# Turning the gated FFN tiles by DMA instead of by TensorE

## The chip, the cores and the metric

The kernel runs on one NeuronCore of one Trainium2 chip. The metric is the device time of one execution in microseconds (us), lower is better; the median of the runs shown is compared. The core has a matrix engine (TensorE, "PE" in the profile, with its weight loads listed apart as "PEld"), VectorE ("DVE"), ScalarE ("ACT"), GpSimd ("POOL"), and SyncE ("SP"), which here only issues DMAs. Sixteen DMA engines move data for all of them. Each engine works through its own instructions in a fixed order and waits at an instruction until that instruction's inputs and output buffer are ready, so what stands behind a waiting instruction on the same engine waits with it.

## The reference

The kernel computes an encoder of two layers on 512 tokens with 1024 channels, float32:

```
for l in range(DEPTH):                                  # DEPTH = 2
    x = x + 0.5 * swiglu(rms_norm(x, ffn1_norm[l]), ffn1_w_in[l], ffn1_w_out[l])
    x = x + mixer(rms_norm(x, mix_norm[l]), ...)
    x = x + 0.5 * swiglu(rms_norm(x, ffn2_norm[l]), ffn2_w_in[l], ffn2_w_out[l])
return rms_norm(x, final_norm)

def swiglu(x, w_in, w_out):
    g, u = jnp.split(x @ w_in, 2, axis=-1)              # D_FF = 2816 columns each
    return (jax.nn.silu(g) * u) @ w_out
```

There are therefore four SwiGLU feed-forward stages (two per layer) and two mixers (neighbourhood attention and a Fourier mix). The change concerns only what lies between `silu(g) * u` and the second product in the four feed-forward stages.

## The kernel before, in words

**Products.** Every float32 matrix is split into a high part (float32r, rounded by a ScalarE copy) and a low part (a VectorE subtraction), and each product is three TensorE products of parts. On top of that the products are done by Strassen's scheme, seven products of quarter matrices (numbered 1 to 7 in the code) in place of eight.

**Weights.** `Stream` walks a list of weight granules of 128 by 1024 floats (512 KB). SP loads a granule into a buffer `raw` (line 147); for some, POOL adds a second granule to it by an accumulating DMA (line 149); VectorE sums pairs for others (line 163). ScalarE then writes the high part `whi` (line 190, or 185 for a negated one) and VectorE the low part `wlo` (line 193 or 186). There are nine `raw` buffers in a feed-forward stage, and three each of `whi` and `wlo`; loads are asked for eight granules ahead, the split two ahead of the product that uses it. A granule serves twelve matmuls in a feed-forward stage.

**A feed-forward stage.** `stage_ffn` has an input half and an output half. The input half goes over the 2816 columns in five blocks of 512 (`for jb in range(...)`; in three of the stages the first block is `first_block`), and one block of 256 columns besides. A block runs the products in the order 1, 5, 6, 2, 7, 3, 4. ScalarE copies partial sums out of PSUM (`snap`, line 560), VectorE subtracts (`less`, line 565), ScalarE takes the tanh (`gate`, line 695), and VectorE multiplies gate and up part (`times`, line 702). The results of a block are two tiles `z2` and `z1`, each [128 tokens, 2 token blocks, 512 columns]: `z2` for tokens 256 to 511, `z1` for tokens 0 to 255. Both are ready only around the last product of the block.

**The turn.** The output half needs the gated values with columns on the partitions. `late_at` remembers each finished `z`. `settle_at` calls `to_at`, which turns a 128 by 128 piece by a TensorE transpose against the identity (line 613), four pieces into one PSUM bank `tr`, and ScalarE copies that bank into an `at` tile (line 617, or line 620 where the two column groups belong to different `at` tiles). One `z` takes eight transposes. In a block of the loop `settle_at` stands between products 1 and 5 (inside `two`), and for the last block after the first product of the output half (`if i == 0`). `at_tile(h, j, c)` gives twelve tiles per stage; `PLACE` says in which one a group of 128 columns goes.

**The output half.** 21 products (`steps`: factors 1 and 2, then 5, 6, 7, 3, and 4, three chunks each) take `at` tiles, or VectorE sums of them (line 715), split into high and low parts by `make`, two steps ahead. VectorE adds the results to `x` (line 721).

**Buffers and order.** Work tiles of 4 KB per partition come from one pool of 23 (`slot`). Outside the blocks marked `manual_schedule`, the order on each engine is fixed before the run by a planner that plays the program through with its own durations: on an engine that is free it places the instruction that comes first in the program among those whose inputs it takes to be ready. On the chip that order then stays as it is, whatever the real durations are. DMAs on SP's and POOL's queues are ordered in the same way.

Of the kernel before, what the change touches and what calls it, by code (L numbers as in the profile page):

```python
# [10 lines left out]
F32R = mybir.dt.float32r  # L11
BF16 = mybir.dt.bfloat16
I32 = mybir.dt.int32
AF = mybir.ActivationFunctionType
ALU = mybir.AluOpType
AX = mybir.AxisListType

P = 128
# [20 lines left out]
PLACE = {f: (h, c, i) for h in range(2) for c in range(3) for i, f in enumerate(CHUNK[h][c])}  # L39
# [50 lines left out]
def encoder_kernel(  # L90
    ctx: ExitStack, tc: tile.TileContext, xin, xtr, wst, gains, gfin, gbias, bias_in, dft, chan, ident_in, rot, out
):
    nc = tc.nc
    V, S, G, PE = nc.vector, nc.scalar, nc.gpsimd, nc.tensor
# [15 lines left out]
    def slot(dt=F32, s="k", shape=(4, 256)):  # L110
        return kp.tile([P, *shape], dt, tag="k", name=nm(s), bufs=23)
# [383 lines left out]
    def product(ps, acts, kts, start, stop=True, again=False, hook=None, by_block=False, ahead=AHEAD):  # L495

        h, l, off = acts
        n = (len(kts) + 1) // 2  # L500

        def granule(i, w, b):
            res = []
            for k, kt in enumerate(kts[2 * i : 2 * i + 2]):
                c, z = slice(off + b * P, off + (b + 1) * P), slice(k * T, (k + 1) * T)
                res.append((
                    ps[b], h[:, kt, c], l[:, kt, c], w[0][:, z], w[1][:, z], start and i + k == 0,
                    stop and 2 * i + k == len(kts) - 1,
                ))
            return res  # L510

        if by_block:
            w = [ws.next() for _ in range(n)]
            for b in range(2):
                for i in range(n):
                    late_low(granule(i, w[i], b), again)
            return
        for i in range(n):
            w = ws.next(AHEAD if i < n - 1 and ahead else ahead)
            if i < n - 1:  # L520
                late_low(granule(i, w, 0) + granule(i, w, 1), again)
            else:
                late_low(granule(i, w, 0), again)
                late_low(granule(i, w, 1), again)
            if hook and i == 0:
                hook()

    def product_T(ps, acts, start):


        h, l, off = acts
        c = slice(off, off + 256)
        wh, wl = ws.next()
        for part in range(2):
            for m in range(2):
                to = ps[:, m * 256 : (m + 1) * 256]
                for k in range(4):
                    z = slice(k * 256 + m * P, k * 256 + (m + 1) * P)
                    if part:
                        PE.matmul(to, wl[:, z], h[:, k, c], start=False, stop=k == 3, skip_group_check=True)  # L540
                    else:
                        one = start and m == 0 and k == 0
                        PE.matmul(to, wh[:, z], h[:, k, c], start=one, stop=False, skip_group_check=True)
                        PE.matmul(to, wh[:, z], l[:, k, c], start=False, stop=False, skip_group_check=True)
# [52 lines left out]
    def stage_ffn(norm, nxt, late):  # L597
# [4 lines left out]
        def at_tile(h, j, c):  # L602
            if (h, j, c) not in at:
                at[h, j, c] = slot(F32, "at")
            return at[h, j, c]
# [42 lines left out]
        if first:  # L648
            for g in range(2):
                w = ws.next()  # L650
# [7 lines left out]
            with tc.manual_schedule(engines={mybir.EngineType.DVE, mybir.EngineType.Activation}):  # L658
# [11 lines left out]
                norm.squares(0, 1)  # L670
                norm.squares(1, 1)
                split(*t4, b21)
        late_at = []
        def plain_out():
            for j in range(2):
                th = slot(F32, "th", (2, 256))
# [10 lines left out]
        def settle_at():  # L687
            while late_at:
                to_at(*late_at.pop(0))
# [9 lines left out]
        def times(z, u, j):  # L699
            for b in range(2):  # L700
                c = 2 * j + b
                V.scalar_tensor_tensor(z[:, b, :], u[b], norm.r2[:, c : c + 1], z[:, b, :], ALU.mult, ALU.mult)
# [64 lines left out]
        def half_times(g, r, u, to, j):  # L767
            V.tensor_tensor(to, u, r, ALU.mult)
            V.tensor_tensor(at_tile(0, j, 0)[:, 0:2, :], g, to, ALU.mult)

        def first_block():

            f0 = 2

            def snap_T(ps):
                t = slot(F32, "sn", (2, 256))
                S.activation(t, ps.rearrange("p (m t) -> p m t", m=2), AF.Copy)
                return t

            def less_T(ps, t):  # L780
                V.tensor_tensor(t, ps.rearrange("p (m t) -> p m t", m=2), t, ALU.subtract)

            pa, ha = pair("A"), bank("hA")
            product(pa, acts[1], K4, True)
            combine(5)
            s1 = snap(pa)
            if len(norm.due) == 2:
                norm.quad(*norm.due.pop(0))
            product_T(ha, acts[1], True)
            h1 = snap_T(ha)  # L790
            pb, hb = pair("B"), bank("hB")
            product(pb, acts[5], K4, True)
            combine(6)
            sb = snap(pb)
            norm.settle()
            product_T(hb, acts[5], True)
            hsb = snap_T(hb)
            norm.rstd()
            norm.spread(R)
            product(pa, acts[6], K4, False, again=True)  # L800
            s2 = snap(pa)
            combine(7)
            product_T(ha, acts[6], False)
            h2 = snap_T(ha)
            pc = pair("C")
            product(pc, acts[2], K4, True)
            less(pc, s1)
            combine(4)
            z1 = gate(s1, 0)
            product(pa, acts[7], K4, False, again=True)  # L810
            hc = bank("hC")
            product_T(hc, acts[2], True)
            less_T(hc, h1)
            r1 = half_gate(h1, 0)
            less(pa, sb)
            product_T(ha, acts[7], False)
            less_T(ha, hsb)
            product(pb, acts[3], K4, False, again=True)
            less(pb, s2)
            z2 = gate(s2, 1)  # L820
            times(z2, [sb[:, 0, :], sb[:, 1, :]], 1)
            product_T(hb, acts[3], False)
            less_T(hb, h2)
            r2 = half_gate(h2, 1)
            half_times(h2, r2, hsb, hsb, 1)
            product(pa, acts[4], K4, False, again=True)
            times(z1, pa, 0)
            product_T(ha, acts[4], False)
            half_times(h1, r1, ha.rearrange("p (m t) -> p m t", m=2), h2, 0)
            late_at.extend([(z2, 1, f0, 4), (z1, 0, f0, 4)])  # L830

        if not first:
            R = slot(F32, "R", (2, T))[:, 0, :]
# [1 line left out]
        for jb in range(0 if first else 1, NB):  # L835
            f0 = 2 + 4 * jb
            if first and jb == 0:
                with tc.manual_schedule(engines={mybir.EngineType.DVE, mybir.EngineType.Activation}):
                    pa = pair("A")
                    product(pa, acts[1], K4, True)  # L840
                    for j in range(2):
                        t = snap(pcl[j])
                        pcl[j] = [t[:, 0, :], t[:, 1, :]]
                    s1 = snap(pa)
                    second(s1)
                    pb = pair("B")
                    product(pb, acts[5], K4, True)
                    sb = snap(pb)
                    norm.rstd()
            else:  # L850
                pa, pb, s1, sb = two(jb)
                settle_at()
            product(pa, acts[6], K4, False, again=True)
            s2 = snap(pa)
            settle_at()
            if jb or not first:
                second(s1)
            else:
                plain_out()
            z1 = gate(s1, 0)  # L860
            product(pa, acts[7], K4, False, again=True)
            less(pa, sb)
            product(pb, acts[3], K4, False, again=True)
            less(pb, s2)
            z2 = gate(s2, 1)
            times(z2, [sb[:, 0, :], sb[:, 1, :]], 1)
            if jb == NB - 1:
                make(0)
                make(1)
            product(pa, acts[4], K4, False, again=True)  # L870
            times(z1, pa, 0)
            late_at += [(z2, 1, f0, 4), (z1, 0, f0, 4)]

        if late or nxt.mix:
            tc.keep_in_program_order(S.activation(small("sq", 1), ones, AF.Sqrt))
# [1 line left out]
        for i, (m, c, _) in enumerate(steps):  # L877
# [13 lines left out]
            )  # L891
            if i == 0:
                settle_at()
            if m == 4 and c == 0 and not late:
                with tc.manual_schedule(engines={mybir.EngineType.DVE, mybir.EngineType.Activation}):
                    make(i + 2)
                    nxt.quad(1, 1)
                    if nxt.mix:
                        nxt.low01 = nxt.quad_high(0, 1)
                    else:  # L900
                        nxt.quad(0, 1)
# [1044 lines left out]
```

## Time and profile before

| | |
|---|---|
| median of 3 runs | 1898.24 us (1897.55 to 1899.96) |
| span of the profiled execution, first to last instruction | 1896.1 us |
| median minus span | 2.1 us |
| mean granted TensorE clock | 0.999 |
| busy share of the span: PE, PEld | 99%, 83% |
| busy share of the span: DVE, ACT, POOL | 87%, 63%, 9% |
| DMA queue of SP / of POOL, share of 16 engines | 41.7% / 28.5% |

Of the profiled execution the profile gives only the span; its own time with what lies around it is not listed, so the median of the runs stands in for it: what lies around the span is taken as 2.1 us. The feed-forward stages lie at about 10 to 337, 605 to 925, 925 to 1265 and 1550 to 1890 us; their input halves end at about 230, 838, 1166 and 1778 us.

How to read it: an engine that is busy all the time sets the end if the others keep it fed. A busy share over the whole span is a mean over stages with different limits, so the tables by stage count more. "Idle before" and the lists of waits say how long an engine sat and whose signal ended it. The chain that ended last is followed backwards from the last instruction: a piece of work on it costs its length, one beside it nothing.

### The profile page before, as it was taken

How to read it: one execution, taken by the hardware profiler on the slowest of the kernel's cores; microseconds unless marked ns; L12 is line 12 of the kernel's file. 1: busy time of each engine (PE TensorE's matmuls, PEld its weight loads, DVE VectorE, ACT ScalarE, POOL GpSimd, SP SyncE). 2: the span in 40 equal slices, each digit the busy share in tenths (PEclk: the TensorE clock that was granted, in tenths of full speed). 3: DMA queues.
4: the chain of work that ended last, by engine and by line, in shares of the span. 5: the costliest groups of instructions: out<-in, count | busy, mean ns of one | idle time of the engine just before them, and what ended most of it. 6: DMA issues, size and time to landing. Idle time of an engine off the chain costs nothing.

```text
span 1896.1 us, 25080 instructions
## 1 busy us (share of the span) xinstructions
PE 1883.8 (99%) x9150; PEld 1578.6 (83%) x9150; DVE 1647.4 (87%) x2006; ACT 1188.6 (63%) x1700; POOL 171.5 (9%) x210
## 2 busy tenths in 40 slices
PE   9999999999999999999999999999999999999998
PEld 7888888888888888888888888888888888888886
DVE  7877899788989987889998778998889899887899
ACT  6655665668665755566665556666685576556664
POOL 0101011100111010001010100101001101100010
PEclk9999999999999999999999999999999999999999
DMA  9777498932886777649867764988248867766594
GB/s 302 208 201 189 152 244 262 230 102 98 242 219 163 183 191 204 178 151 258 254 193 202 194 174 154 267 267 213 84 137 229 215 169 177 207 177 178 173 278 143
DMA packets 106940, 372.75 MB, mean 197 GB/s; under 512 B 12288, under 2 KB 12416, under 8 KB 106816
## 3 DMA queue, kind: packets, MB, share of 16 engines
q1 hardware_dynamic: 78144, 272.80, 41.7%
q0 software_dynamic: 28528, 98.33, 28.5%
q8 instruction: 72, 1.18, 0.2%
q14 instruction: 52, 0.43, 0.1%
q10 hardware_dynamic: 144, 0.02, 0.0%
HBM read 365.85 MB, written 2.11 MB: 194 GB/s over the span
## 4 chain that ended last, share of the span: by engine, by line
PE 96%; DMA 1%; DVE 1%; issue 1%; SPq 0%; ACT 0%; POOL 0%; DVEq 0%; POOLq 0%; ACTq 0%
PE A L490 10%; PE A L491 10%; PE A L493 10%; PE o L493 7%; PE o L490 7%; PE o L491 7%; PE B L490 5%; PE B L491 5%; PE B L493 5%; PE ps L314 4%; PE ps L315 4%; PE ps L316 3%; PE C L491 2%; PE C L490 2%; PE C L493 2%; PE tr L613 2%
## 5 line engine op out<-in xcount | busy, mean ns | idle before, releaser
L190 ACT ACTIVATE whi<-raw 128x1024 fp32r<-128x1024 f32 (+1 forms) x534 | 551.4, 1037 | 388.5 <-PE A L491 124.2
L193 DVE TENSOR_TENSOR wlo<-raw,whi 128x1024 fp32r<-128x1024 f32 (+1 forms) x534 | 633.3, 1192 | 167.7 <-ACT whi L190 166.4
L149 POOL DMA_DIRECT2D raw<-in_wst_dram x166 | 144.4, 899 | 1369.9 <-DMA raw<-in_wst_dram 927.9
L163 DVE TENSOR_TENSOR raw<-raw,raw 128x1024 f32<-128x1024 f32 (+1 forms) x150 | 177.4, 1190 | 1.2
L490 PE MATMUL A<-whi,xh 128*128 128x512 f32 x400 | 155.7, 389 | 0.0
L491 PE MATMUL A<-whi,xl 128*128 128x512 f32 x400 | 155.7, 389 | 0.0
L493 PE MATMUL A<-wlo,xh 128*128 128x512 f32 x400 | 115.1, 389 | 0.0
L185 ACT ACTIVATE whi<-raw 128x1024 fp32r<-128x1024 f32 (+1 forms) x83 | 85.8, 1037 | 42.2 <-PE o L491 14.0
L186 DVE SCALAR_TENSOR_TENSOR wlo<-raw,whi 128x1024 fp32r<-128x1024 f32 (+1 forms) x83 | 98.0, 1194 | 12.7 <-ACT whi L185 12.7
L695 ACT ACTIVATE th<-sn,rh 128x512 f32<-128x512 f32 x80 | 56.9, 715 | 69.7 <-DVE sn L565 69.7
L560 ACT ACTIVATE sn<-A 128x512 f32<-128x512 f32 x104 | 60.8, 589 | 45.8 <-PE A L493 45.7
L493 PEld LDWEIGHTS A<-wlo,xh 128*128 128x128 f32 x400 | 75.1, 188 | 15.6
L491 PEld LDWEIGHTS A<-whi,xl 128*128 128x128 f32 x400 | 75.1, 188 | 15.4
L490 PEld LDWEIGHTS A<-whi,xh 128*128 128x128 f32 x400 | 75.1, 188 | 15.4
L490 PE MATMUL C<-whi,xh 128*128 128x512 f32 x208 | 81.2, 390 | 0.0
L491 PE MATMUL C<-whi,xl 128*128 128x512 f32 x208 | 81.0, 389 | 0.0
L490 PE MATMUL B<-whi,xh 128*128 128x512 f32 x208 | 81.0, 389 | 0.0
L491 PE MATMUL B<-whi,xl 128*128 128x512 f32 x208 | 81.0, 389 | 0.0
L493 PE MATMUL C<-wlo,xh 128*128 128x512 f32 x208 | 59.8, 389 | 0.0
L493 PE MATMUL B<-wlo,xh 128*128 128x512 f32 x208 | 59.8, 389 | 0.0
L490 PE MATMUL B<-whi,t5h 128*128 128x512 f32 x136 | 54.3, 399 | 0.0
L715 DVE TENSOR_TENSOR at<-at,at 128x1024 f32<-128x1024 f32 (+1 forms) x48 | 53.7, 1127 | 0.0
(448 smaller groups left out, 4786.0 us busy)
## 6 DMA issues: line engine op xcount, KB each, us to landing
raw<-in_wst_dram SPq DMA_DIRECT2D x470, 512.0 KB, 5.4
raw<-in_wst_dram POOLq DMA_DIRECT2D x174, 512.0 KB, 8.1
raw<-in_wst_dram SPq DMA_DIRECT2D x30, 256.0 KB, 4.1
bm<-in_bias_dram SPq DMA_DIRECT2D x16, 384.0 KB, 3.8
vs<-v SPq DMA_DIRECT2D x12, 256.0 KB, 3.8
x<-in_xin_dram SPq DMA_DIRECT2D x4, 512.0 KB, 10.2
raw<-in_wst_dram POOLq DMA_DIRECT2D x8, 256.0 KB, 8.2
dft<-in_dft_dram POOLq DMA_DIRECT2D x8, 256.0 KB, 4.4
```

The source lines that it names most:

```text
L149: G.dma_start(out=self.t, in_=wst[GRAN_AT[self.plus]][:, 0 : self.n], accum_op=ALU.add)
L163: V.tensor_tensor(self.raw.t, self.raw.t, self.add.t, ALU.add)
L185: S.activation(hi, t, AF.Copy, scale=-1.0)
L186: self.last = V.scalar_tensor_tensor(lo, t, -1.0, hi.bitcast(F32), ALU.mult, ALU.subtract)
L190: S.activation(hi[:, cs], t[:, cs], AF.Copy)
L193: self.last = V.tensor_tensor(lo[:, cs], t[:, cs], hi[:, cs].bitcast(F32), ALU.subtract)
L314: PE.matmul(ps, lh, rh, start=start, stop=False, skip_group_check=again)
L315: PE.matmul(ps, lh, rl, start=False, stop=False, skip_group_check=again)
L490: PE.matmul(ps, lh, rh, start=start, stop=False, skip_group_check=again)
L491: PE.matmul(ps, ll, rh, start=False, stop=False, skip_group_check=again)
L493: PE.matmul(ps, lh, rl, start=False, stop=stop, skip_group_check=again)
L560: S.activation(t[:, b, :], ps[b], AF.Copy)
```

## The change

A tile `z` is no longer turned by TensorE. `halves` lets ScalarE copy the tile twice, once the lower 16 bits of every word and once the upper 16 bits, into a tile `zs` of 16-bit integers; one transposing DMA on SP's queue turns all of `zs` (128 by 2048 of 16 bits, 512 KB) into `zt`. `joined` later lets ScalarE write the two halves from `zt` back into the words of the `at` tiles, two copies for each run of column groups that lie side by side in one `at` tile. The four groups of a `z` are one run in four of the five blocks, and two runs (one group and three) in the block with column groups 10 to 13.

`halves` is called as soon as a `z` is finished. `joined` is called twice in the next block: after product 5, and after the copy of product 6's sum. For the last block it is called after the second and the fourth product of the output half, `z1` first. The small block of 256 columns in the first stage is still turned by TensorE (eight transposes).

```diff
+U16 = mybir.dt.uint16
...
-        late_at = []
+        late_at, turned = [], []
+
+        def halves(z, j, f0):
+
+            s, t = slot(U16, "zs", (2, 4, 2, P)), slot(U16, "zt", (2, 4, 256))
+            words = z.bitcast(U16).rearrange("p b (q f h) -> p h q b f", q=4, h=2)
+            for h in range(2):
+                S.activation(s[:, h], words[:, h], AF.Copy)
+            nc.sync.dma_start_transpose(
+                out=t.rearrange("p h q (b t) -> p (h q b) t", b=2), in_=s.rearrange("p h q b f -> p (h q b f)")
+            )
+            turned.append((t, j, f0))
+
+        def joined():
+
+            t, j, f0 = turned.pop(0)
+            q = 0
+            while q < 4:
+                h, c, i = PLACE[f0 + q]
+                n = 1
+                while q + n < 4 and PLACE[f0 + q + n] == (h, c, i + n):
+                    n += 1
+                to = at_tile(h, j, c).bitcast(U16).rearrange("p i (t w) -> p w i t", w=2)
+                for w in range(2):
+                    S.activation(to[:, w, i : i + n, :], t[:, w, q : q + n, :], AF.Copy)
+                q += n
...
             half_times(h2, r2, hsb, hsb, 1)
+            halves(z2, 1, f0)
             product(pa, acts[4], K4, False, again=True)
             times(z1, pa, 0)
+            halves(z1, 0, f0)
             product_T(ha, acts[4], False)
             half_times(h1, r1, ha.rearrange("p (m t) -> p m t", m=2), h2, 0)
-            late_at.extend([(z2, 1, f0, 4), (z1, 0, f0, 4)])
...
                 pa, pb, s1, sb = two(jb)
                 settle_at()
+                joined()
             product(pa, acts[6], K4, False, again=True)
             s2 = snap(pa)
             settle_at()
+            if turned:
+                joined()
...
             times(z2, [sb[:, 0, :], sb[:, 1, :]], 1)
+            halves(z2, 1, f0)
...
             times(z1, pa, 0)
-            late_at += [(z2, 1, f0, 4), (z1, 0, f0, 4)]
+            halves(z1, 0, f0)
...
             if i == 0:
                 settle_at()
+            if i == 1:
+                turned.reverse()
+                joined()
+            if i == 3:
+                joined()
```

## The prediction

> **What bounds the kernel now.** I read the busy shares first, then TensorE's waits, the chain that ended last, and the table by stage.
>
> ```profile
> span 1896.1 us, 25080 instructions
> PE 1883.8 (99%) x9150; PEld 1578.6 (83%) x9150; DVE 1647.4 (87%) x2006; ACT 1188.6 (63%) x1700; POOL 171.5 (9%) x210
> ...
> PE ps L135 <- DVE ones L131: 1.2, 1, 1.2
> PE A L490 <- ACT sn L560: 1.0, 1, 1.0
> PE cl L490 <- ACT whi L190: 0.5, 1, 0.5
> PE o L493 <- DVE wlo L193: 0.4, 1, 0.4
> PE cl L493 <- DVE wlo L193: 0.3, 1, 0.3
> ```
>
> These five lines are all of TensorE's waits: 3.4 us. TensorE sets the end nearly everywhere, so a transpose taken off it is worth its full length, as long as the others keep it fed. In the chain, the transposes of line 613 appear as 20 pieces (first, second, one from the middle, last):
>
> ```profile
> 72.28 2.62 PE tr L613 x24
> 113.00 1.75 PE tr L613 x16
> ...
> 1054.82 1.75 PE tr L613 x16
> ...
> 1784.86 1.75 PE tr L613 x16
> ```
>
> By stage (the four input halves, one block of 40 us in the third of them, two output halves):
>
> ```profile
> core 0: us, PE busy (x) PEld busy (x) DVE busy (x) ACT busy (x) POOL busy (x), PEclk, DMA share, GB/s
> 15.00:240.00 225.00, 224.73 (x1035) 186.65 (x1034) 183.15 (x204) 139.98 (x190) 19.10 (x22) 1.00 0.69 202
> 612.00:840.00 228.00, 228.00 (x1130) 193.23 (x1129) 187.54 (x203) 140.70 (x189) 18.47 (x22) 1.00 0.68 182
> 925.00:1190.00 265.00, 265.00 (x1302) 224.31 (x1301) 224.00 (x244) 163.22 (x214) 21.99 (x26) 1.00 0.68 191
> 1560.00:1800.00 240.00, 240.00 (x1188) 203.49 (x1187) 200.56 (x217) 147.55 (x190) 19.37 (x23) 1.00 0.66 182
> ...
> 1049.00:1089.00 40.00, 40.00 (x186) 33.39 (x185) 30.63 (x32) 22.66 (x29) 3.41 (x4) 1.00 0.72 193
> ...
> 840.00:925.00 85.00, 85.00 (x389) 70.67 (x389) 84.92 (x88) 52.86 (x63) 10.35 (x12) 1.00 0.87 246
> 1190.00:1285.00 95.00, 95.00 (x437) 79.05 (x436) 91.05 (x94) 60.58 (x82) 10.88 (x13) 1.00 0.91 274
> ```
>
> In an input half ScalarE is busy 57 to 62% and the DMA engines about 68%: room for what the change adds. In an output half VectorE is as full as TensorE (84.92 of 85 us), and 4 of the 20 batches stand there.
>
> **Step 1, TensorE.** Removed are 20 batches of 16 transposes; the small block's 8 stay. 20 x 1.75 = 35.0 us leave the chain. In the 16 batches inside input halves nothing else is near its limit, so 28.0 us are gained whole. In the output halves VectorE takes over: the gain of the other 7.0 us lies between 0 (VectorE cannot go faster) and 7.0 (its lead over TensorE absorbs it). As both are at 100%, neither row is nearer, and I take half: 3.5 us.
>
> **Step 2, ScalarE's work.**
>
> ```profile
> L190 ACT ACTIVATE whi<-raw 128x1024 fp32r<-128x1024 f32 x506 | 533.9, 1060 | 381.6 <-PE A L491 124.2 <-DVE raw L163 56.3 <-PE o L491 52.4
> L617 ACT ACTIVATE at<-tr 128x512 f32<-128x512 f32 x74 | 38.8, 608 | 0.0
> L357 ACT ACTIVATE junk<-x 128x512 bf16<-128x512 f32 x56 | 34.7, 619 | 3.1 <-DVE x L721 1.9 <-DVE x L1755 1.1
> L620 ACT ACTIVATE at<-tr 128x256 f32<-128x256 f32 x16 | 5.3, 398 | 0.0
> L320 ACT ACTIVATE c1h<-at 128x768 fp32r<-128x768 f32 x1 | 0.8, 833 | 0.0
> ```
>
> Removed: 72 of the 74 copies of line 617 (two are the small block's) and all 16 of line 620: 72 x 0.608 + 16 x 0.398 = 50.1 us. Added per tile, of 40: two copies of 1024 elements in `halves`; two of 1024 in `joined`, or in 8 of the 40 two of 256 and two of 768. No row copies 16-bit words with a stride. The one with a 16-bit output (619 ns for 512 elements) costs as much as the 32-bit one (608), so I go by element count: 80 x 1.06 + 64 x 1.06 + 16 x (0.398 + 0.833) = 172.3 us. If a strided 16-bit copy ran at twice that, it would be 345; a 16-bit copy at half price would be 86. Net +122 us, ScalarE at 1311 of about 1861 us, 70%. In the 40 us block it is 22.7 + 122 / 20 = 28.8 of 38.2 us, 75%: in the mean it fits, so I cost it at nothing, covered by ScalarE's idle time. At twice the price the block needs 37.4 of 38.2 and the cover is gone.
>
> **Step 3, where ScalarE stands still.** A `joined` waits on ScalarE for its DMA; behind it in the same stream stand the `whi` copies, then VectorE's `wlo`, then TensorE. How long may ScalarE be late?
>
> ```profile
> 1051.23 1.06 ACT L190 ACTIVATE whi<-raw 128x1024 fp32r<-128x1024 f32 x1 [1.16 <-PE A L491]
> ...
> 1051.94 0.39 PE L490 MATMUL A<-whi,xh 128*128 128x512 f32 x1
> ...
> 1054.66 1.91 PE L613 MATMUL tr<-ident,th 128*128 128x128 f32 x16
> 1056.33 0.48 PE L490 MATMUL B<-whi,t5h 128*128 128x512 f32 x1
> ...
> 1059.14 0.39 PE L490 MATMUL B<-whi,t5h 128*128 128x512 f32 x1
> ...
> 1049.79 1.41 DVE L702 SCALAR_TENSOR_TENSOR th<-A,r,th 128x512 f32<-128x512 f32 x2
> ```
>
> The copy at 1051.23 waited for TensorE to free the buffer. With three buffers it serves the third granule from there (1051.94, 1056.33, 1059.14). It ended at 1052.29, so 6.85 us early; without the transposes in between, 5.1 us. A `whi` may thus come 5.1 us late at no cost. A `joined` itself takes 2.1 us, so it may wait 3.0 us more than the plan took it to. `z1` is ready at 1051.2; its `joined` stands in the program after product 6, some 20 us later, but the planner puts it wherever it takes ScalarE to be free and the DMA to have landed. So the cover is not the 20 us but the planner's accuracy. What the DMA really takes no row shows; the nearest:
>
> ```profile
> raw<-in_wst_dram SPq DMA_DIRECT2D x470, 512.0 KB, 5.4
> raw<-in_wst_dram POOLq DMA_DIRECT2D x174, 512.0 KB, 8.1
> vs<-v SPq DMA_DIRECT2D x12, 256.0 KB, 3.8
> row<-r POOLq DMA_DIRECT2D x5, 2.0 KB, 9.6
> ...
> q1 hardware_dynamic: 78144, 272.80, 41.7%
> q0 software_dynamic: 28528, 98.33, 28.5%
> ```
>
> Landing lies between 3.8 us (`vs`, buffer to buffer on chip, half the size) and 9.6 us (`row`, whose words are scattered singly). I take 5.4 us, the row of the same size and queue. Against a plan as short as 3.8 that is 1.6 us late, under 3.0: no cost. At 9.6 it is 5.8 late: 2.8 us of TensorE for each `joined`, 112 us over 40.
>
> **Step 4, the queues.**
>
> ```profile
> SPq L147 <- DVE wlo L193: 900.0, 295, 19.7
> ...
> ACT whi L190 <- DMA raw<-in_wst_dram: 19.3, 12, 3.0
> ```
>
> SP gains 40 issues, each of which waits for ScalarE's second copy; the weight loads of line 147 queue behind, and the accumulating loads of POOL (line 149) and `whi` wait for those. SP spends 900 us of the span waiting for `raw` buffers to come free, and ScalarE waits for weights 19.3 us in all, so the loads land ahead of need; I cost it at nothing. If that cover went, it would show in the second row. Engine time: SP's queue moved 272.80 MB in 41.7% of 1896.1 us, which is 1.5 us of all 16 engines per 512 KB; POOL's accumulating loads come to 2.9. 40 transposes at 1.5 to 2.9 us are 61 to 115 us. Free in the four input halves are 0.31 x 225 + 0.32 x 228 + 0.32 x 265 + 0.34 x 240 = 309 us, or 7.7 us for each transpose.
>
> One rule speaks against this. The Trainium skill, "VectorE: DVE Perf Modes", section "The three transpose paths", lists 1309 ns for turning one 128 by 128 block of 16 bits by DMA. If the 16 blocks of one tile follow one another, that is an estimate of 20.9 us. Its page "Advanced Engine Details and Errata", "X-Bar Transpose (TRN2)", has transposing DMAs as fast as plain ones, which would be the 1.5 us above. No run here shows either yet; the first is the last rival below.
>
> **Step 5, buffers.** `zs` and `zt` take two of the 23 slots where `z` held one; `z` comes free as soon as it is halved. A shortage would delay a copy as in step 3. The PSUM banks of `tr` come free, which gains nothing, since TensorE waits for no bank. Both at 0.
>
> **The sum.** 1896.1 - 28.0 - 3.5 = 1864.6 us of span. The median of the runs stands 2.1 us above the profiled span: 1866.7, predicted 1867.
>
> **Rivals.**
> - *Partly eaten.* VectorE bounds the output halves (0 of 7.0 us gained), and ScalarE holds TensorE for 0.85 us in each of the 20 pairs of joins: 1898.2 - 28.0 + 17 = 1887. For it: VectorE's 84.92 of 85 us. Against: 5.1 us of slack.
> - *No change.* The holds cost about 1.4 to 1.8 us in each of 20 pairs (31.5 / 20 = 1.6), and the saving is gone: within 3.8 us of 1898 (0.2%, about what a measurement of this kernel can tell from no change).
> - *Slower: ScalarE blocks at `joined`.* The transposes land later than planned, `whi` comes more than 5.1 us late, and TensorE stops. It decides from 3.0 + 31.5 / 40 = 3.8 us beyond plan. At 9.6 us landing: 112 us if all 40 joins pay, 56 us if one of each pair does: 1923 to 1979. For it: ScalarE is strictly in order, and the DMA share is 0.66 to 0.72, so a transpose queues behind weights. Against: weights landing in 5.4 us in the same crowd.
> - *Slower: the transposes fill the DMA engines.* It decides above 7.7 us of engine time each, 40 us for each us beyond; at the 9.6 us of `row`, 40 x 1.9 = 76 us: 1943. Against: 1.5 and 2.9 us per 512 KB for both kinds of load. By the skill's 1309 ns it would be 40 x (20.9 - 7.7) = 528 us, some 2395 us, as an estimate.
>
> **Chances.** The forecast 0.53 (its own range 1860 to 1877: all of the output halves gained, to 10 us of holds); partly eaten 0.12; no change 0.06; ScalarE blocks 0.24; DMA engines full 0.05. So faster 0.65, same 0.06, slower 0.29. The range reaches up to 1930: it takes in the forecast, both middle cases and about half of the blocking case, and leaves out some 0.12 + 0.05 above and little below.
>
> **What would show it.** Right: line 613 is left with 8 transposes; TensorE's waits stay near 3 us; ScalarE's new copies take about 1.06 us; the 40 transposes land in about 5 us; ScalarE's waits for them stay below 3 us each. Wrong: waits of TensorE for `whi` or `wlo` in the input halves, with ScalarE before them waiting for the transposing DMA; ScalarE's waits for weights far above 19.3 us with a DMA share near 1 (engines full); or VectorE near 100% in the input halves too.

## The result, and the profile after

| | median of the runs | beside the kernel before |
|---|---|---|
| before | 1897.89 us (1896.17 to 1899.96) | |
| after | 1890.14 us (1888.10 to 1892.10) | ratio 0.9959, 95% interval 0.9945 to 0.9973 |

The changed kernel is faster by 7.75 us. The direction was forecast, the size was not: 31 us had been expected, and three quarters of it are missing.

The profiled execution after, first its page (span, busy shares, SP's DMA queue), then all waits of TensorE that reach 0.5 us:

```profile
span 1890.3 us, 24637 instructions
PE 1860.5 (98%) x8830; PEld 1549.5 (82%) x8830; DVE 1641.4 (87%) x2006; ACT 1310.0 (69%) x1788; POOL 171.3 (9%) x210
...
q1 hardware_dynamic: 161344, 293.77, 48.6%
```

```profile
PE o L491 <- ACT c1h L321: 13.5, 4, 3.4
PE C L491 <- ACT whi L191: 4.3, 4, 2.3
PE ps L136 <- DVE ones L132: 1.2, 1, 1.2
PE A L491 <- ACT sn L561: 0.9, 1, 0.9
PE o L492 <- DVE c1l L322: 0.5, 2, 0.3
```

TensorE has the 320 instructions fewer (9150 to 8830), but its busy time fell by 23.3 us and not by 35.0, and a wait that the kernel before did not have stands on top: four times 3.4 us for `c1h`, ScalarE's high part of the first factor of the output half. There are four feed-forward stages, and the four waits lie at their four turns from the input half to the output half. The table by stretches of 5 us shows one of them:

```profile
core 0: us, PE busy (x) PEld busy (x) DVE busy (x) ACT busy (x) POOL busy (x), PEclk, DMA share, GB/s
220.00:225.00 5.00, 1.63 (x9) 1.01 (x7) 4.06 (x7) 3.75 (x5) 0.00 (x0) 1.00 0.54 193
225.00:230.00 5.00, 5.00 (x14) 3.65 (x15) 4.97 (x5) 4.97 (x6) 0.00 (x0) 0.66 1.04 243
230.00:235.00 5.00, 5.00 (x24) 4.13 (x22) 4.97 (x6) 4.21 (x5) 0.00 (x0) 1.00 0.67 176
```

TensorE stands still for most of the first stretch. In the second it is "busy" all the time, but starts 14 products where it usually starts 24, at a granted clock of 0.66. This is why the busy time fell too little: the wait is followed by some us of slow matmuls that count as busy. Who is ahead of `c1h`? The timelines of ScalarE, TensorE and VectorE at the last turn:

```profile
1765.35 0.73 ACT L722 ACTIVATE th<-sn,rh 128x512 f32<-128x512 f32 x1 [1.93 <-DVE sn L566]
...
1771.02 1.06 ACT L186 ACTIVATE whi<-raw 128x1024 fp32r<-128x1024 f32 x1 [2.54 <-PE A L492]
1771.98 1.99 ACT L681 ACTIVATE zs<-th 128x1024 uint16<-128x1024 uint16 x2
1773.88 1.78 ACT L321 ACTIVATE c1h<-at 128x768 fp32r<-128x768 f32 x2
1775.56 1.99 ACT L681 ACTIVATE zs<-th 128x1024 uint16<-128x1024 uint16 x2
...
1770.77 0.61 PE L494 MATMUL A<-wlo,xh 128*128 128x512 f32 x2
1774.76 1.22 PE L491 MATMUL o<-whi,c1h 128*128 128x512 f32 x2 [3.37 <-ACT c1h L321]
...
1769.93 1.41 DVE L729 SCALAR_TENSOR_TENSOR th<-sn,r,th 128x512 f32<-128x512 f32 x2
```

`c1h` needs `at` tiles of earlier blocks only. In the kernel before ScalarE wrote it ahead of the turn, here in the third stage, where the first product of the output half starts at 1168.76 us:

```profile
1163.51 0.83 ACT L320 ACTIVATE c1h<-at 128x768 fp32r<-128x768 f32 x1
1164.25 1.04 ACT L185 ACTIVATE whi<-raw 128x1024 fp32r<-128x1024 f32 x1
1165.19 0.71 ACT L695 ACTIVATE th<-sn,rh 128x512 f32<-128x512 f32 x1
...
1168.76 0.39 PE L490 MATMUL o<-whi,c1h 128*128 128x512 f32 x1
```

There `c1h` starts 5.25 us ahead of its product, between the two tanh (`th`) of `z2`. After the change there is no `c1h` in that place, behind the tanh at 1765.35; it comes behind the copies of `halves(z2)`, although ScalarE stood idle for 2.54 us shortly before them. In the program `halves(z2, 1, f0)` now stands ahead of `make(0); make(1)`.

How late is that? The product at 1774.76 had waited 3.37 us, so it was due at 1771.39, and `c1h` starts 2.5 us after that. Measured from the matmuls it starts 7.7 us later than before. Only 1.9 of these are the copies themselves (1771.98 to 1773.88). They need `z2`, which VectorE finishes at 1771.34 (the VectorE line), and behind them `c1h`, which needs no `z2`, has to wait for it too. Why the planner did not put `c1h` into the idle time is not shown; the expectation of run 1 names the work buffers, which would be given out in program order.

What the transposing DMA and the new copies cost, by the view of the tile `zt` and by the groups of ScalarE's instructions:

```profile
L682 SPq DMA_TRANSPOSE zt<-zs x40: 1844/3562/6708, 73.1 to 1778.0; - x40
...
  DMA zt<-zs: 17.5, 11
...
DMA to landing us min/median/max: 4.4/5.7/9.4
```

```profile
L698 ACT ACTIVATE at<-zt 128x1024 uint16<-128x1024 uint16 x64 | 86.5, 1367 | 1.6 <-DMA zt<-zs 1.5
L681 ACT ACTIVATE zs<-th 128x1024 uint16<-128x1024 uint16 x80 | 79.6, 1043 | 0.4 <-DVE th L729 0.4
L698 ACT ACTIVATE at<-zt 128x768 uint16<-128x768 uint16 x16 | 16.5, 1072 | 0.0
L698 ACT ACTIVATE at<-zt 128x256 uint16<-128x256 uint16 x16 | 7.9, 491 | 16.0 <-DMA zt<-zs 16.0
```

**An account of what TensorE loses.** Successive 512-column matmuls start 0.227 us apart when nothing holds them. For each run I added up, over all pairs of matmuls that start more than 0.25 us apart, what lies above 0.227. This takes waits and slow matmuls together. The kernel before loses 12.5 us in this way, the kernel after 40.2: 27.7 us more. Of these, 5.4, 5.8, 5.6 and 5.3 us, together 22.1, lie at the four turns (where before lost less than 0.4 each). Against the 35.0 us of transposes taken away that leaves 7.3, beside the 7.75 measured. The other 5.6 us lie mostly at joins inside blocks: 4.2 at one of them, at 1095 us.

### The profile page after: what moved, and what is told of

The parts are those of the page before. It is cut to its first block, busy times and chain, and to the rows that moved or that the text cites. A ratio compares the mean times of both kernels' runs of the same rounds, so it can differ in the third digit from the quotient of the medians.

```text
span 1890.3 us, 24637 instructions
## 1 busy us (share of the span) xinstructions
PE 1860.5 (98%) x8830; PEld 1549.5 (82%) x8830; DVE 1641.4 (87%) x2006; ACT 1310.0 (69%) x1788; POOL 171.3 (9%) x210
## 3 DMA queue, kind: packets, MB, share of 16 engines
q1 hardware_dynamic: 161344, 293.77, 48.6%
## 5 line engine op out<-in xcount | busy, mean ns | idle before, releaser
L698 ACT ACTIVATE at<-zt 128x1024 uint16<-128x1024 uint16 (+2 forms) x96 | 110.9, 1172 | 17.7 <-DMA zt<-zs 17.5
L681 ACT ACTIVATE zs<-th 128x1024 uint16<-128x1024 uint16 x80 | 79.6, 1043 | 0.4 <-DVE th L729 0.4
```

The source lines that it names most:

```text
L681: S.activation(s[:, h], words[:, h], AF.Copy)
L698: S.activation(to[:, w, i : i + n, :], t[:, w, q : q + n, :], AF.Copy)
```

## The experiments

All are compared with runs of the kernel before on the same chip; its medians there were 1898.07, 1897.25 and 1898.77 us, in the order of the three groups 1 to 4, 5 to 8 and 9 to 10. The last two columns of this table are the account just described: saved transposes (1.75 us per batch of 16) against what TensorE loses beyond the kernel before.

| run | change of the median | ratio, 95% interval | saved | lost | lost minus saved |
|---|---|---|---|---|---|
| after | -7.75 | 0.9959 (0.9945 to 0.9973) | 35.0 | 27.7 | -7.3 |
| 1 make first | -14.5 | 0.9917 (0.9900 to 0.9935) | 35.0 | 17.9 | -17.1 |
| 2 zt in z | -9.6 | 0.9945 (0.9926 to 0.9963) | 35.0 | 22.3 | -12.7 |
| 3 last block on TensorE | -25.7 | 0.9861 (0.9841 to 0.9881) | 28.0 | 0.9 | -27.1 |
| 4 joins pinned | -9.8 | 0.9944 (0.9926 to 0.9961) | 35.0 | 23.1 | -11.9 |
| 5 only the last block by DMA | +16.7 | 1.0088 (1.0073 to 1.0103) | 7.0 | 22.0 | +15.0 |
| 6 before with copies | +22.7 | 1.0121 (1.0105 to 1.0136) | 0 | 21.2 | +21.2 |
| 7 each DMA twice | +12.6 | 1.0057 (1.0040 to 1.0074) | 28.0 | 40.4 | +12.4 |
| 8 pinned, last block on TensorE | -27.2 | 0.9855 (0.9841 to 0.9870) | 28.0 | -1.4 | -29.4 |
| 9 join copies twice | +28.3 | 1.0151 (1.0132 to 1.0170) | 28.0 | 54.8 | +26.8 |
| 10 half of the last block by DMA | -28.5 | 0.9846 (0.9830 to 0.9863) | 31.5 | 1.4 | -30.1 |

The account follows the medians to within 3.1 us in every run. TensorE has work for nearly the whole span, so a sum over its starts has to come out close; what the account adds is the places at which the time is lost.

**1. The first factor ahead of the copies.** The two calls of `make` are moved in front of `halves(z2)`; nothing else changes.

```diff
-            halves(z2, 1, f0)
             if jb == NB - 1:
                 make(0)
                 make(1)
+            halves(z2, 1, f0)
```

> Only the program order changes: the two calls of make (the first c1h copies of the output half) stand ahead of halves of the last block's z2. Theory A (place in the program: the planner gives work buffers in program order, so c1h queues behind the halving copies of z2 and TensorE runs dry at each of the four turns to the output half): TensorE's waits for c1h fall from 13.5 us to under 1 us, the clock is granted in full there, time falls by about 20 us to 1870. Theory B (too few work buffers, 23): the waits stay, 1890. Theory C (ScalarE has too much work or waits for the transposing DMA): 1888 to 1890.

Measured: 1883.58 us (1881.42 to 1884.31). `c1h` is back ahead of the turn, as ScalarE's timeline shows (the first product of the output half starts there at 1762.51 us), and the four waits for it are gone:

```profile
1757.26 0.83 ACT L321 ACTIVATE c1h<-at 128x768 fp32r<-128x768 f32 x1
...
1763.93 2.01 ACT L681 ACTIVATE zs<-th 128x1024 uint16<-128x1024 uint16 x2 [0.57 <-DVE th L729]
```

```profile
PE C L491 <- ACT whi L191: 4.1, 3, 1.6
PE o L491 <- ACT c2h L321: 2.3, 3, 0.9
PE o L494 <- DVE wlo L194: 1.4, 2, 0.7
...
PE o L492 <- DVE c1l L322: 1.1, 3, 0.4
PE o L492 <- DVE c2l L322: 1.0, 3, 0.5
```

So the order of the program set the wait. But only some 7 us came back where 20 had been expected: 17.9 us are still lost. Of these 8.0 lie at the four turns, now in many small waits for the next factors (`c1l`, `c2h`, `c2l`), 4.9 at three joins inside blocks, and 3.7 in the last output half, where TensorE waited for `wlo`. Mending the one wait lets the next in line show.

**2. One buffer less.** The DMA writes its result back into `z`, whose content is dead by then, so that each tile takes two buffers instead of three.

```diff
-            s, t = slot(U16, "zs", (2, 4, 2, P)), slot(U16, "zt", (2, 4, 256))
+            s = slot(U16, "zs", (2, 4, 2, P))
+            t = z.rearrange("p b f -> p (b f)").bitcast(U16).rearrange("p (h q t) -> p h q t", h=2, q=4)
```

> The transposing DMA writes back into the tile z, which halves has just read, so each tile in flight holds one work buffer less; nothing else changes. Theory A (program order): c1h still queues behind the halving copies, TensorE's waits for c1h stay at about 13.5 us, time stays at about 1890. Theory B (buffer shortage): the waits go, about 1870. Theory C: about 1890.

Measured: 1888.48 us (1886.73 to 1890.01), and the wait for `c1h` is what it was, 13.5 us in four. It is not a buffer for `c1h` that is late.

**3. The last block of each stage on TensorE.** Four blocks of each stage keep the DMA, the fifth is turned as in the kernel before.

```diff
-            halves(z2, 1, f0)
+            if jb < NB - 1:
+                halves(z2, 1, f0)
...
-            halves(z1, 0, f0)
+            if jb < NB - 1:
+                halves(z1, 0, f0)
+            else:
+                late_at += [(z2, 1, f0, 4), (z1, 0, f0, 4)]
...
-            if i == 1:
-                turned.reverse()
-                joined()
-            if i == 3:
-                joined()
```

> The last block of each stage is turned by TensorE as before (64 of the 320 transposes come back), the other four blocks by DMA. Theory A and B alike: the four waits at the turn to the output half go with their slow clock (20 us less), four batches of 1.75 us come back (7 us more): about 1877. Theory C (the cost lies with ScalarE and the DMAs in every block): four fifths of the gain of after, about 1891 or 1892.

Measured: 1872.33 us (1871.59 to 1873.98). With 64 transposes more on TensorE the kernel is some 18 us faster than after, and 5 us faster than expected. The largest of TensorE's waits that are left:

```profile
PE C L491 <- ACT whi L191: 1.3, 2, 0.8
```

The 16 batches inside the input halves give their 28.0 us nearly whole, and without the last block next to nothing is lost (0.9 us by the account). This includes the 4.2 us at the join at 1095 us, which is inside a block: the planner orders the whole program anew for each run, so a run does not change one place alone.

**4. The joins kept in program order.** The planner may not move the copies of `joined`.

```diff
-                    S.activation(to[:, w, i : i + n, :], t[:, w, q : q + n, :], AF.Copy)
+                    tc.keep_in_program_order(S.activation(to[:, w, i : i + n, :], t[:, w, q : q + n, :], AF.Copy))
```

> The copies of joined keep their place in the program on ScalarE: the planner may not float them ahead. Theory A: the four waits for c1h stay (13.5 us); ScalarE's 17.5 us of waits for the transposing DMA and TensorE's 4.3 us of waits for whi in product 2 go, with the one slow stretch of the clock inside a block: 4 to 6 us less than after, about 1885. Theory C (ScalarE's waits for the DMA are what eats the gain): 1865 to 1870.

Measured: 1888.24 us (1887.02 to 1889.46), 1.9 us below after, which the intervals do not separate, where 4 to 6 had been expected. ScalarE no longer waits for the DMA, TensorE's 4.3 us of waits for `whi` are gone, the 13.5 us for `c1h` stay. So ScalarE blocking at `joined` was real, but small.

**5. The opposite half: only the last block by DMA.** The first four turned blocks of each stage go back to TensorE; the last one is halved, turned and joined as in the changed kernel.

```diff
-            halves(z2, 1, f0)
             if jb == NB - 1:
+                halves(z2, 1, f0)
                 make(0)
                 make(1)
...
-            halves(z1, 0, f0)
+            if jb == NB - 1:
+                halves(z1, 0, f0)
+            else:
+                late_at += [(z2, 1, f0, 4), (z1, 0, f0, 4)]
```

> Opposite half of the change: the first four turned blocks of each stage stay with TensorE, and only the last block goes by the transposing DMA (8 of 40 transposes), in the changed kernel's order (halves ahead of make). Theory of the turn (the loss lies where c1h stands behind the zs copies: 3.5 us of wait and some 2 us of slow clock at each of four turns): 4 x 1.75 = 7.0 us less TensorE work, 4 x 5.5 = 22 us lost, so 15 us slower than before, 1913 us (1908 to 1919). Rival, the loss is spread over all 40 transposes (27.7 us of wider matmul spacing, a fifth of it here): 7.0 saved less 5.5 lost, 1896 us.

Measured: 1913.91 us (1913.22 to 1916.36), as the theory of the turn had it (1913). This fifth of the change alone makes the kernel slower by 0.9%, through the same wait:

```profile
PE o L491 <- ACT c1h L321: 13.5, 4, 3.4
```

**6. The kernel before, with the copies alone.** All TensorE transposes stay, no transposing DMA is issued, nothing reads the copies.

```diff
+        def copies(z):
+            s = slot(U16, "zs", (2, 4, 2, P))
+            words = z.bitcast(U16).rearrange("p b (q f h) -> p h q b f", q=4, h=2)
+            for h in range(2):
+                S.activation(s[:, h], words[:, h], AF.Copy)
...
             if jb == NB - 1:
+                copies(z2)
                 make(0)
                 make(1)
             product(pa, acts[4], K4, False, again=True)
             times(z1, pa, 0)
+            if jb == NB - 1:
+                copies(z1)
```

> The kernel before, all 320 TensorE transposes kept, with only the eight pairs of zs copies of the last blocks added on ScalarE, in the place where the changed kernel has them; nothing reads the copies and no transposing DMA is issued. 8 x 2 x 1.04 = 17 us of ScalarE work in all. Theory of the turn: c1h again comes behind two copies, TensorE waits some 3.4 us and then runs at a low clock, 4 x 5.5 = 22 us: 1920 us (1912 to 1924). Rival, the DMA's traffic or its write into SBUF makes the slow clock or the wait: no DMA, so 1898 to 1902 us and no granted clock under 0.95 at the turns. Between them (1908 to 1912): the wait of 3.4 us alone costs, and the clock stays up.

Measured: 1919.96 us (1919.15 to 1922.91). Sixteen copies, 17 us of work on an engine that is busy 63% of the time, cost 22.7 us. The wait is the same, and so is the first turn by stretches of 5 us:

```profile
PE o L491 <- ACT c1h L321: 13.5, 4, 3.4
```

```profile
225.00:230.00 5.00, 1.68 (x8) 1.06 (x6) 4.09 (x6) 3.68 (x5) 0.00 (x0) 1.00 0.51 185
230.00:235.00 5.00, 4.95 (x17) 4.00 (x18) 4.93 (x5) 4.98 (x6) 0.00 (x0) 0.66 0.27 105
```

The wait and the clock of 0.66 are there without any transposing DMA (DMA share 0.27). So neither the DMA's traffic nor its write into SBUF makes them; the copies of `z2` ahead of `c1h` do, and run 1 says that it is by their place and not by their work.

**7. Each transposing DMA twice.** On the kernel of run 3.

```diff
             nc.sync.dma_start_transpose(
                 out=t.rearrange("p h q (b t) -> p (h q b) t", b=2), in_=s.rearrange("p h q b f -> p (h q b f)")
             )
+            nc.sync.dma_start_transpose(
+                out=t.rearrange("p h q (b t) -> p (h q b) t", b=2), in_=s.rearrange("p h q b f -> p (h q b f)")
+            )
```

> On the kernel whose last blocks are turned by TensorE (1872.3 us): each of the 32 transposing DMAs is issued twice in a row, into the same buffer. Adds 32 x 3.6 = 115 us of hold on SP's queue and 32 x 3.3 = 106 us of 16 engines; the landing that ScalarE waits for goes from 5.7 to some 9.3 us. Theory that queue and engines have room and that the joins have slack of about 5 us: 1872 to 1877 us. Rival, ScalarE blocks at the joins or weights come late: 32 x 3.6 = up to 115 us more if all of it shows, 1900 us if a quarter does.

Measured: 1909.89 us (1905.46 to 1912.31), 38 us above run 3 by the changes against before (12.6 and -25.7). My theory, that there is room, missed; a third of the doubled DMA's 115 us shows. The waits of ScalarE and TensorE, and one of the joins on ScalarE's timeline with what TensorE then waited for:

```profile
ACT at L701 <- DMA zt<-zs: 65.0, 16, 6.0
...
PE C L491 <- ACT whi L191: 15.4, 10, 2.5
PE A L491 <- ACT whi L191: 10.5, 11, 1.0
```

```profile
125.63 2.55 ACT L701 ACTIVATE at<-zt 128x1024 uint16<-128x1024 uint16 x2 [5.47 <-DMA zt<-zs]
128.06 1.03 ACT L191 ACTIVATE whi<-raw 128x1024 fp32r<-128x1024 f32 x1
...
129.14 0.50 PE L491 MATMUL C<-whi,xh 128*128 128x512 f32 x1 [1.99 <-ACT whi L191]
```

ScalarE stands 5.47 us at the join, the `whi` behind it comes late, and TensorE waits 1.99: here ScalarE had about 5.47 - 1.99 = 3.5 us of room. Weights that come late are not what costs here, since ScalarE's own waits for them rose only from 14.5 us in run 3 to 18.5; the order on ScalarE passed the delay on. One landing of 5.7 us is covered, two in a row are not.

**8. Runs 3 and 4 together.** The edits are the two shown there.

> The last blocks on TensorE and the joins kept in program order, both at once. If the two gains add (25.7 us and 2 us): 1870 us (1868 to 1872). If the 2 us of the pinning were the block turns that the first edit has already mended: 1872 us as without it.

Measured: 1870.07 us (1869.27 to 1871.23). This beats both kernels: 1.45% below before where the changed kernel is 0.41% below. The 1.5 us to run 3 are within the intervals.

**9. Each join copy twice.** On the kernel of run 3.

```diff
                 for w in range(2):
-                    S.activation(to[:, w, i : i + n, :], t[:, w, q : q + n, :], AF.Copy)
+                    for _ in range(2):
+                        S.activation(to[:, w, i : i + n, :], t[:, w, q : q + n, :], AF.Copy)
```

> On the kernel whose last blocks are turned by TensorE (1872.3 us): each join copy on ScalarE is made twice, 80 more copies, 86 us more ScalarE work (67% to some 73% of the span) with the same transposing DMAs. Theory that ScalarE has room for its work and only what stands ahead of a weight piece in its order costs: between 1873 and 1890 us, because each join now holds ScalarE 2.7 us longer just before weight pieces that TensorE needs; the lower end if the pieces are ahead by that much, as the 13.2 us that ScalarE already waited at eight joins without a loss suggest. Rival, ScalarE's work counts one for one: 1872 + 86 = 1958 us.

Measured: 1927.03 us (1924.70 to 1932.75). Against run 3 that is 28.3 + 25.7 = 54 us where the added copies raised ScalarE's busy time by 72.6 us (1284.4 to 1357.0, 70% of the span): both expectations missed, the truth lies between. TensorE's waits, a product that came late, and a second join on ScalarE's timeline with the late product behind it:

```profile
PE A L491 <- ACT whi L191: 34.4, 16, 2.8
```

```profile
135.06 0.80 PE L491 MATMUL A<-whi,t3h 128*128 128x512 f32 x1 [2.37 <-ACT whi L191]
...
212.32 4.97 ACT L699 ACTIVATE at<-zt 128x1024 uint16<-128x1024 uint16 x4
217.14 1.99 ACT L191 ACTIVATE whi<-raw 128x1024 fp32r<-128x1024 f32 x2
...
218.23 0.50 PE L491 MATMUL A<-whi,t3h 128*128 128x512 f32 x1 [2.36 <-ACT whi L191]
```

Two copies of a join take 2.55 us, four take 4.97: 2.42 us more, and 2.36 arrive at TensorE. But the first join of the block is doubled too, so 4.84 us were added ahead of this product, and the room before it was some 2.5 us. Run 3 shows the same: in its second block the first of the two `whi` behind the second join ends at 125.4, 2.1 us ahead of its product.

```profile
124.36 2.00 ACT L191 ACTIVATE whi<-raw 128x1024 fp32r<-128x1024 f32 x2
...
127.56 0.39 PE L491 MATMUL A<-whi,t3h 128*128 128x512 f32 x1
```

The changed kernel has the same 2.1 us there, and 0.6 in the next block, whose joins have four copies. So ScalarE has room, but not for another join.

**10. Half of the last block by DMA.** On the kernel of run 8: `z2` of the last block goes by DMA, with `make` ahead of `halves(z2)` as in run 1; `z1` stays with TensorE.

```diff
             if jb == NB - 1:
                 make(0)
                 make(1)
+            halves(z2, 1, f0)
...
+            else:
+                late_at += [(z1, 0, f0, 4)]
```

> On the best kernel so far (1870.1 us, joins pinned): of the last block of each stage one of the two tiles (z2) goes by the transposing DMA too, with c1h ahead of its copies, and z1 stays with TensorE. 4 batches less on TensorE. If the matmul saving shows: 1870.1 - 7.0 x 4/8 = 1866.6 us. If VectorE paces the stretch behind the turn (it is busy 40.0 of 40 us there), the saving turns into waits: 1869 to 1872 us. If the added ScalarE copies delay c2h or the weights as in the first experiment: 1874 to 1877 us.

Measured: 1870.26 us (1868.20 to 1870.88), not to be told from run 8: against before the two differ by 1.3 us, which the intervals separate neither from 0 nor from the 3.5 us saved. By the account 2.8 of the 3.5 are lost again. In run 8 VectorE has no idle moment behind the third turn, and in run 10 the largest of TensorE's waits that run 8 does not have is for VectorE, in the last output half:

```profile
1160.00:1190.00 30.00, 30.00 (x138) 24.94 (x137) 30.00 (x34) 18.96 (x27) 3.44 (x4) 1.00 0.91 237
```

```profile
PE o L494 <- DVE wlo L194: 1.2, 2, 0.7
```

This agrees with VectorE pacing the output half; that nothing else holds it there was not tried.

## Why the prediction was right or wrong

**Step 1, TensorE: right in the input halves, wrong at the turn.** Run 3 gives 25.7 us of the 28.0. For the output halves I took 3.5 of 7.0 us, as a guess halfway. Runs 8 and 10 show no gain that can be measured from the first 3.5 of the 7.0. With both tiles of the last block the kernel is slower than without (-14.5 in run 1 against -25.7 in run 3): there the turns cost more than they save.

**Step 2, ScalarE's work: the total right, the reading of it wrong. Here the prediction failed.** Net 121.4 us were added (1188.6 to 1310.0) where 122 was forecast. The copies of `halves` took 1.043 us against 1.06; the copies of `joined`, which write 16-bit words with a gap, 1.367 against 1.06, 1.072 against 0.833 and 0.491 against 0.398. But I costed all of it "at nothing, covered by ScalarE's idle time", because a block of 40 us had 25% of idle time left. The cover was a mean. At the turn the two copies of `halves(z2)` came ahead of `c1h`, which TensorE waits for, and four turns cost 22.1 us. Their 2.0 us of work are the smaller part; behind them `c1h` had to wait for `z2`, which it does not need. Run 6 shows that price with the copies alone, and run 1 takes the wait away by the order alone. I had asked what stands behind a `joined` on ScalarE, and never what stands behind a `halves`: the diff shows that `make(0); make(1)` does.

**Step 3, ScalarE standing still: the landing right, the slack right at some joins and too large at others.** The landing was forecast at 5.4 us and was 5.7 (4.4 to 9.4). ScalarE stood 17.5 us at eleven joins, at most 3.4, and TensorE lost 4.3 us of waits for `whi`. Of the 17.5 us 16.0 stand ahead of the copies of 256 elements, so in the block whose joins have four copies, and there too lie all four of TensorE's waits; the prediction had read its slack in another block. The slack of 5.1 us, 3.0 after a join, came from one `whi` copy which had waited for its buffer, that is, from a place where ScalarE was as far ahead as it can be. Run 7 measured about 3.5 us left at a first join, the changed kernel about 2.1 behind a second one and 0.6 in the block with four copies. That the conclusion held is in part luck: the landing came in near plan.

**Step 4, the queues: right that they cost nothing, the size a little low.** SP's queue went from 41.7% of 1896.1 us to 48.6% of 1890.3: 128.0 us, or 3.2 for each transposing DMA, where 1.5 to 2.9 had been estimated and 7.7 were free. ScalarE's waits for weights went from 19.3 to 17.9 us. By the 1309 ns for a block of 128 by 128 (the Trainium skill, "VectorE: DVE Perf Modes", "The three transpose paths") 16 blocks one after another would be 20.9 us for a tile, as an estimate; the trace does not agree: a tile of 16 blocks lands 5.7 us after issue.

**Step 5, buffers: right.** Run 2 takes one away per tile and leaves the wait as it was.

**The rivals.** "Partly eaten" gave 1887 and lies nearest in number, by another mechanism: not 0.85 us at each pair of joins, but 5.5 us at each turn. "ScalarE blocks at `joined`" came to 4.3 us of waits in the changed kernel, where 56 to 112 had been named, but run 7 shows that it stands close by: with the landing doubled, half of the 32 joins wait and the saving is more than gone. "DMA engines full" did not happen. No rival named the turn.

**Corrected sum.** 1896.1 - 35.0 + 27.7 = 1888.8 us of span, with 1890.3 in the profile. Of the 27.7, 22.1 us are the turns, and most of the rest waits for `whi` at joins; the last 1.5 us the account does not place.

## What to carry to other kernels

A busy share, even of one block, does not cover added work on an engine that works strictly in order: follow each added instruction to the instruction that the planner or the program puts behind it, and ask who waits for that, and what the added one itself waits for. Turns between stages need a look of their own, since there the lead that a steady stretch builds up is spent. And where a change applies at many places, put it in place by place: here four fifths of it brought 25.7 us, and the last fifth took most of that away.

## What the runs showed of the hardware

**A stop of TensorE of 3.4 us costs about half as much again.** After each of the 3.4 us waits of the changed kernel the matmuls started 0.43 us apart instead of 0.227 for some us, with a granted clock of 0.66 to 0.68 over 5 us, which added 1.8 to 2.3 us to the stop. In the runs 1, 3 and 8 no stop after the first 12 us was longer than 1.8 us, and no matmuls 0.43 us apart followed one. In between the length does not decide. Run 9 has eleven stops of about 2.4 us; six were followed by the slow spacing, five were not. Two of them, 2.37 us at 135.06 and 2.36 us at 218.23, were followed by

```profile
135.00:140.00 5.00, 4.94 (x15) 3.96 (x16) 4.78 (x5) 4.19 (x6) 0.00 (x0) 0.66 0.85 210
...
218.00:223.00 5.00, 4.77 (x21) 3.96 (x22) 4.79 (x5) 4.25 (x6) 0.00 (x0) 1.00 0.44 145
```

a slow clock in the one case and the full clock in the other. The Trainium skill, "TensorE: Matmul & The Clock Gate", "Part 1: The HAM clock gate (the "warmup" mystery)", describes a window of about 3.4 us that runs on by itself, and a clock that is halved after at least one window in which TensorE was idle. The spacing of 0.43 us agrees with the half clock, and a window that runs on by itself could be why two equal stops ended differently; but a stop of 2.4 us was enough here, shorter than a whole window.

**A transposing DMA holds its queue.** Its issue occupied SP for 1.8 to 6.7 us, 3.6 us in the median, where that of a weight load (line 148) took 0.33 us in the median. A tile of 512 KB took 2080 packets ((161344 - 78144) / 40).

**A copy that writes every other 16-bit word is slower than one that reads so.** For 1024 elements ScalarE took 1.367 us against 1.043.
